# Third recurrence unit in flight, longer stretches between chain looks, norms of the recurrence output on chip: one fp32 four-layer kernel

## The chip, the cores and the metric

One NeuronCore of one Trainium2 chip runs the whole program. The metric is the device time of one execution in microseconds (us); the kernel before was run three times, and its median stands below. TensorE is called PE, VectorE DVE, ScalarE ACT, GpSimd POOL and SyncE (which issues the DMAs) SP, as in the profile.

## The reference, cut to what matters

The input has 512 tokens of width 1024. Two "first" layers are followed by two "second" layers. The change touches the first layers alone, so only these are shown.

```python
for l in range(2):
    h = rmsnorm(x, norm1_g[l])
    p = h @ w_in[l]                       # rw, ret, sg, gate columns
    y_rw  = rwkv7_branch(p_rw, ...)       # recurrence over 512 steps, 8 heads of 64
    y_ret = retention_branch(p_ret, cos, sin)
    y_sg  = sgu_branch(p_sg, ...)
    proj  = einsum('bsgc,gcd->bsgd', stack([y_rw, y_ret, y_sg]), w_branch[l])
    gates = sigmoid(gate_logits)
    x = x + sum(gates * proj, over the branches) @ w_out[l]
    x = x + conv_ffn(rmsnorm(x, norm2_g[l]), ...)

# rwkv7_branch: per step and head
#   S = S diag(w_t) - (S kk_t)(a_t kk_t)^T + v_t k_t^T ;  y_t = S r_t
# and behind it, per head of 64 columns:
y = (y - mean) * rsqrt(var + 64e-5) * lnx_g + lnx_b
y = y + sum(r * k * r_k) * v
y_rw = y * g
# retention_branch ends with, per head of 128 columns:
y = y * rsqrt(mean(y * y) + 1e-6);  y_ret = y * silu(g)
```

## The kernel before

Everything lies features on partitions: a tile is 128 features by 512 tokens. Every projection is a sum over blocks of 128 input features, and every such block is three matmuls (`mm3`, L165 to L170): operands are split into a high and a low part, and high by high, low by high and high by low are summed in PSUM. `weights` (L151 to L161) loads 512 KB of weights (`wraw`, two buffers); ACT makes the high part (`whi`, L159) and DVE the low part (`wlo`, L160). One tile of 1024 input features is 8 blocks, 24 matmuls of 512 columns. Weight tiles that must come out with tokens on partitions go through `tm_group` (L379): four token groups of 256 columns, each needing both halves (chunks) of the weights.

The order of PE's work in the mixing stage of a first layer is written by hand. `Plan` (L68 to L103) keeps threads, Python generators that emit instructions and yield a `Step` with a cost and a wait in a model time. A dense thread (rank 1: input projections, rank 2: retention and gating unit, rank 3: the merge gates) is taken when no chain thread is due; chain threads (rank 0) carry the recurrence and interrupt a dense tile wherever it yields `MORE`. Before, `fm_steps` (L369) yields it after every second block. On the other engines a scheduler orders the work; weight splits and PSUM evacuations have priority, and what stands in `late()` is issued only behind the last evacuation.

The recurrence is done in this way. `rw_pair` (L465) makes the key, decay and rate tiles of one pair of heads; it sums squares (`psk`), sends the sums through DRAM to spread them over the partitions (`sums`, L196: four small matmuls, a copy, a DMA out, two DMAs back), and goes on with `kkr` (L523 or L529) and the products `psA` (L542). `rwkv_inverse` solves small triangular systems on DVE. Then 16 units follow (4 pairs of 4 chunk groups, `rw_unit` L610): transposes `pst`, products `psam`, which DVE masks into `am` (L652, four instructions), `psv`, `psg`, `psh` and `rhs` (L670), `psu`, then `psy` and `psx`. Two `lane` threads (L594) take units from one list, so two units are in flight, each with tiles of its own. Behind the last unit of a pair comes `rw_final` (L706): a scan over six steps (`psz`, L719 and L721), `psY`, then the mean and the reciprocal root of the variance. Both of these go through `sums` and DRAM (`psmean`, `psq`, names `sumd` and `rdw` in the trace), and the result is scaled, shifted, gated (`psgate`, L747) and split into the tiles that the merge reads (`split`, L181 and L182).

Retention (L761) rotates q and k (`ev`, `swp`; `swp` is filled by four DMAs), and per head makes `pssc`, `pret`, `psret`, and a norm `psrn` whose sums go through DRAM too; `ret_end` (L822) multiplies `yret` by the spread result `sqr`.

PSUM has 8 banks: 2 for dense tiles (`pm`), 4 for the recurrence (`pw`), 2 for retention and gating (`pf`). `merge` (L923) runs after the plan: for every block c of 128 output features it multiplies the three branch outputs (n = 0 retention, 1 gating unit, 2 recurrence, by `ORDER1`) with their weights (`pbr`, 12 matmuls a tile), and gates them (L939). The weight stream has the same order (`merge_stream`, L1907).

Of the kernel before, what the change touches and what calls it, by code (L numbers as in the profile page):

```python
# [45 lines left out]
LANES = 2  # L46
# [13 lines left out]
def Dense(cost):  # L60
    return Step(cost)


MORE = Step(1.4, inner=True)
TILE = Dense(1.4)


class Plan:  # L68
# [38 lines left out]
class Kern:  # L107
# [262 lines left out]
    def fm_steps(self, ws):  # L370

        ps = self.PM(name="pm")
        for k in range(KD):
            self.mm3(ps, next(ws), self.h[k], k == 0, k == KD - 1)
            if k % 2 and k < KD - 1:
                yield MORE
        return ps

    def tm_group(self, src, evac):  # L379

        ws = [self.weights(src[i], 1024) for i in range(2)]
        for g in range(4):
            ps = self.PM([128, 512])
            for k in range(KD):
                w = ws[k // 4]
                o = (k % 4) * 256
                hh = (self.h[k][0][:, g * 128:(g + 1) * 128], self.h[k][1][:, g * 128:(g + 1) * 128])
                self.mm3(ps[:, :256], hh, (w[0][:, o:o + 256], w[1][:, o:o + 256]), k == 0, k == KD - 1)
                if k == KD // 2 - 1:
                    yield MORE  # L390
            evac(g, ps[:, :256])
            yield MORE if g < 3 else TILE

# [191 lines left out]
    def rwkv_out(self, l):  # L585
# [4 lines left out]
        self.states, self.left, self.ended = {}, [4] * 4, [False] * 4  # L590
        for i in range(LANES):
            self.plan.add(self.lane(l, i), 0, 2.0 * i)

    def lane(self, l, i):  # L594

        while self.units:
# [7 lines left out]
            yield from self.rw_unit(f, g, self.states[f], i)  # L604
# [4 lines left out]
    def rw_unit(self, f, g, st, lane):  # L609
# [8 lines left out]
        small = lambda shape, name: self.ap.tile(shape, F32, name=name, tag=name, bufs=LANES)  # L618
# [6 lines left out]
        tk = small([128, 2, 128], "tk")  # L625
        nc.vector.tensor_copy(tk, pst[:, 1:3, :])
        vp = self.vp[lane]
        nc.scalar.activation(vp[:, 0:4:3, :], pst[:, 3, :].rearrange("p (e v) -> p e v", e=2), AF.Copy)
        rhs = small([128, 2, 128], "rhs")
        nc.scalar.activation(rhs[:, 0, 64:128], pst[:, 0, 0:64], AF.Copy, scale=-1.0)  # L630
        nc.scalar.activation(rhs[:, 1, 0:64], pst[:, 0, 64:128], AF.Copy, scale=-1.0)
        tt = small([128, 2, 4, 32], "tt")
# [6 lines left out]
        am = self.am[lane]  # L639
# [13 lines left out]
        yield Chain(1.4, 4.0)  # L653
# [10 lines left out]
        gs_ = small([128, 2, 128], "gsb")  # L664
# [6 lines left out]
        yield Chain(0.5, 2.5)  # L671
# [3 lines left out]
        uw = small([128, 2, 128], "uw")  # L675
# [31 lines left out]
    def rw_final(self, l, f, st):  # L707
# [16 lines left out]
        for c in range(1, 8):  # L724
            cs = slice(64 * c, 64 * c + 64)
            for e in range(2):
# [7 lines left out]
        mean = flat(st["cc"])  # L734
# [13 lines left out]
        gt = mean  # L748
# [1326 lines left out]
```

## Time and profile before

| what | us |
|---|---|
| runs, median of 3 (lowest, highest) | 3331.58 (3329.52, 3349.09) |
| the profiled execution, by the same clock | 3336.96 |
| its span in the trace | 3335.3 |
| first merge matmul (`pbr`) of first layer 0, in the trace | 499.34 |
| first merge matmul of first layer 1, in the trace | 1473.06 |

The span is the time between the first and last recorded instruction of the profiled execution. Busy time of an engine counts its instructions alone, not the issue of DMAs. A row of the timeline gives the start, the duration, the engine, the line, the operation with output and input tiles, the shape, a count of like instructions, and in brackets the idle time ahead of it with what ended it. PE's instructions overlap, so the pace is read from the distance of starts, not from durations.

### The profile page before, as it was taken

How to read it: one execution, taken by the hardware profiler on the slowest of the kernel's cores; microseconds unless marked ns; L12 is line 12 of the kernel's file. 1: busy time of each engine (PE TensorE's matmuls, PEld its weight loads, DVE VectorE, ACT ScalarE, POOL GpSimd, SP SyncE). 2: the span in 40 equal slices, each digit the busy share in tenths (PEclk: the TensorE clock that was granted, in tenths of full speed). 3: DMA queues.
4: the chain of work that ended last, by engine and by line, in shares of the span. 5: the costliest groups of instructions: out<-in, count | busy, mean ns of one | idle time of the engine just before them, and what ended most of it. 6: DMA issues, size and time to landing. Idle time of an engine off the chain costs nothing.

```text
span 3335.3 us, 47337 instructions
## 1 busy us (share of the span) xinstructions
PE 3245.5 (97%) x17944; PEld 2596.1 (78%) x17944; DVE 2194.4 (66%) x4062; ACT 1365.3 (41%) x2440; POOL 116.7 (3%) x139
## 2 busy tenths in 40 slices
PE   8999999999999999999999999999999999999998
PEld 6787877888887687878888877876787888777776
DVE  6765656777437755656677456986666669866665
ACT  5433433444335333434444334344334443543343
POOL 0000000000000000000000000010003100100031
PEclk9999999999999999999999999999999999999999
DMA  4433245332433323245333436453455554544464
GB/s 146 124 93 93 79 136 173 124 103 96 136 110 107 120 78 89 83 147 176 101 96 103 146 115 195 141 155 98 120 185 195 171 165 130 156 114 122 150 208 141
DMA packets 200244, 435.41 MB, mean 131 GB/s; under 512 B 29768, under 2 KB 57800, under 8 KB 200016
## 3 DMA queue, kind: packets, MB, share of 16 engines
q1 hardware_dynamic: 200016, 432.38, 41.9%
q8 instruction: 142, 2.33, 0.3%
q14 instruction: 86, 0.70, 0.1%
HBM read 339.57 MB, written 61.49 MB: 120 GB/s over the span
## 4 chain that ended last, share of the span: by engine, by line
PE 85%; DVE 6%; DMA 5%; ACT 2%; issue 1%; SPq 1%; POOL 0%; DVEq 0%; ACTq 0%; POOLq 0%
PE pm L168 22%; PE pm L170 21%; PE pm L169 21%; PE psy L1152 2%; PE pbr L168 2%; PE pbr L169 2%; PE pbr L170 2%; PE pspt L1142 2%; DVE wlo L160 2%; PE psl L1124 1%; DMA rdw<-sumd 1%; PE psl L1125 1%; DMA sqr<-sumd 1%; PE pssc L804 1%; DMA zd<-z 1%
## 5 line engine op out<-in xcount | busy, mean ns | idle before, releaser
L168 PE MATMUL pm<-shi,whi 128*128 128x512 f32 x3072 | 1234.6, 402 | 8.5 <-ACT whi L159 7.4
L170 PE MATMUL pm<-shi,wlo 128*128 128x512 f32 x3072 | 1211.5, 394 | 2.3 <-DVE wlo L160 2.2
L169 PE MATMUL pm<-slo,whi 128*128 128x512 f32 x3072 | 1210.9, 394 | 0.9 <-DVE slo L185 0.9
L159 ACT ACTIVATE whi<-wraw 128x1024 fp32r<-128x1024 f32 x480 | 508.4, 1059 | 887.8 <-PE pm L169 579.0
L160 DVE TENSOR_TENSOR wlo<-wraw,whi 128x1024 fp32r<-128x1024 f32 x480 | 588.7, 1226 | 203.3 <-ACT whi L159 199.4
L168 PEld LDWEIGHTS pm<-shi,whi 128*128 128x128 f32 x3072 | 579.2, 189 | 150.0 <-issue 26.8
L170 PEld LDWEIGHTS pm<-shi,wlo 128*128 128x128 f32 x3072 | 578.9, 188 | 131.1 <-DVE wlo L160 6.8
L169 PEld LDWEIGHTS pm<-slo,whi 128*128 128x128 f32 x3072 | 579.6, 189 | 119.2 <-issue 4.3
L424 DVE TENSOR_TENSOR ev<-pm,rb 128x512 f32<-128x512 f32 x140 | 96.1, 686 | 112.7 <-PE pm L170 112.2
L894 DVE TENSOR_TENSOR gate<-pm,rb 128x512 f32<-128x512 f32 x80 | 55.1, 689 | 121.6 <-PE pm L170 121.3
L168 PE MATMUL pbr<-shi,whi 128*128 128x512 f32 x288 | 116.6, 405 | 12.2 <-ACT shl L181 9.6
L168 PE MATMUL pm<-whi,shi 128*128 128x256 f32 x384 | 115.0, 300 | 10.0 <-ACT whi L159 10.0
L169 PE MATMUL pm<-wlo,shi 128*128 128x256 f32 x384 | 112.0, 292 | 4.8 <-DVE wlo L160 4.8
L170 PE MATMUL pbr<-shi,wlo 128*128 128x512 f32 x288 | 114.3, 397 | 0.0
L169 PE MATMUL pbr<-slo,whi 128*128 128x512 f32 x288 | 114.3, 397 | 0.0
L170 PE MATMUL pm<-whi,slo 128*128 128x256 f32 x384 | 111.6, 291 | 0.0
L939 DVE SCALAR_TENSOR_TENSOR gate<-gate,pbr 128x512 f32<-128x512 f32 x128 | 85.8, 683 | 37.5 <-PE pbr L170 36.3
L943 POOL TENSOR_TENSOR gate<-gate 128x512 f32<-128x512 f32 x48 | 77.4, 1613 | 607.7 <-DVE gate L939 343.8
L936 ACT ACTIVATE gate<-gate 128x512 f32<-128x512 f32 x128 | 75.7, 625 | 42.6 <-DMA gate<-gtd 39.6
L1109 ACT ACTIVATE p<-psl,st 128x256 f32<-128x256 f32 (+3 forms) x128 | 64.9, 511 | 51.6 <-DVE st L1107 44.1
L168 PEld LDWEIGHTS pm<-whi,shi 128*128 128x128 f32 x384 | 76.0, 198 | 12.9 <-ACT whi L159 10.7
L169 PEld LDWEIGHTS pm<-wlo,shi 128*128 128x128 f32 x384 | 76.4, 199 | 6.2 <-DVE wlo L160 5.7
(483 smaller groups left out, 4461.3 us busy)
## 6 DMA issues: line engine op xcount, KB each, us to landing
wraw<-in_w_gt SPq DMA_DIRECT2D x148, 512.0 KB, 3.7
wraw<-in_w_in SPq DMA_DIRECT2D x116, 512.0 KB, 3.6
wraw<-in_f_up SPq DMA_DIRECT2D x88, 512.0 KB, 3.5
gtd<-gate SPq DMA_DIRECT2D x116, 256.0 KB, 2.0
gate<-gtd SPq DMA_DIRECT2D x116, 256.0 KB, 4.0
wraw<-in_w_br SPq DMA_DIRECT2D x44, 512.0 KB, 3.6
wraw<-in_f_dn SPq DMA_DIRECT2D x44, 512.0 KB, 3.5
wraw<-in_w_out SPq DMA_DIRECT2D x32, 512.0 KB, 3.9
```

The costliest lines, as they stand in the source:

```text
L159: nc.scalar.activation(hi[:, :n], raw[:, :n], AF.Copy)
L160: nc.vector.tensor_tensor(lo[:, :n], raw[:, :n], hi[:, :n].bitcast(F32), op=OP.subtract)
L168: nc.tensor.matmul(ps, lhsT=lhs[0], rhs=rhs[0], start=first, stop=False, skip_group_check=skip)
L169: nc.tensor.matmul(ps, lhsT=lhs[0], rhs=rhs[1], start=False, stop=False, skip_group_check=skip)
L170: nc.tensor.matmul(ps, lhsT=lhs[1], rhs=rhs[0], start=False, stop=last, skip_group_check=skip)
L424: self.last = self.nc.vector.tensor_tensor(t, ps, self.rb, op=OP.mult)
L936: nc.scalar.activation(g, g, AF.Tanh, scale=0.5)
L939: nc.vector.scalar_tensor_tensor(g, g, 1.0, pb, op0=OP.add, op1=OP.mult)
L943: (nc.gpsimd if self.pre and n in self.cfg.get("pa", (1, 2, 3)) else nc.vector).tensor_tensor(g, g, acc, op=OP.add)
L1109: nc.scalar.activation(p[:, :w], l, AF.Exp, bias=st[:, 0:1], accum_out=st[:, 1:2])
L1142: nc.tensor.transpose(pt_[:, b * 128:(b + 1) * 128], ps[e][:, b * 128:(b + 1) * 128], self.ident)
L1152: nc.tensor.matmul(psy[64 * e:64 * e + 64, :], lhsT=vs[e][b], rhs=pts[e][:, b * 128:(b + 1) * 128], start=first and b == 0, stop=last and ...
```

## The change

It does nine things, all in the first layers.

1. `LANES` is 3. The third lane's tiles come from tiles that are free by then (tags C4 and R); POOL zeroes two of them. Lanes start 0, 10 and 20 us apart in the plan's model time, not 0 and 2.
2. `fm_steps` yields `MORE` once, after four blocks, and `MORE` and `TILE` count 2.75, not 1.4.
3. A chain thread is taken up to 0.8 us (`NEAR`) before it is due.
4. Some of a unit's waits in the plan are shorter (4.0 to 3.2, 2.5 to 2.0, 2.5 to 2.2).
5. Two pairs of ACT copies into `rhs` become one copy each.
6. `tm_group` works chunk by chunk: all four groups with the first half of the weights, then all with the second. Two groups share a PSUM bank, and both `pm` banks are held all along.
7. `rw_final` norms on the chip: two matmuls with 64 equal weight columns put the sums on all partitions at once (`psm`, 512 columns each), four small ones make the sums of squares (`psq`, 2 columns), ACT and DVE make the reciprocal root of 8 columns (`hcol`), and eight matmuls spread it (`rows`, 64 by 128). Two round trips through DRAM are gone, and three DVE instructions behind the root become two.
8. The wait behind `psm` is 3.0 where the two waits behind the trips were 10.0 and 11.0.
9. The merge takes branch 2 of block c behind branches 0 and 1 of block c+1, and the weight stream follows.

```diff
-LANES = 2
+LANES = 3
-MORE = Step(1.4, inner=True)
-TILE = Dense(1.4)
+MORE = Step(2.75, inner=True)
+TILE = Dense(2.75)
+NEAR = 0.8
...
-            due = sorted((th for th in self.threads if th["chain"] and th["due"] <= self.t), key=lambda th: th["due"])
+            due = sorted((th for th in self.threads if th["chain"] and th["due"] <= self.t + NEAR), key=lambda th: th["due"])
...
-            if k % 2 and k < KD - 1:
+            if k == KD // 2 - 1:
                 yield MORE
...
     def tm_group(self, src, evac):
-        ws = [self.weights(src[i], 1024) for i in range(2)]
-        for g in range(4):
-            ps = self.PM([128, 512])
-            for k in range(KD):
...
+        ps = [self.PM([128, 2, 256]) for _ in range(2)]
+        for i in range(2):
+            w = self.weights(src[i], 1024)
+            for g in range(4):
+                for k in range(4):
...
+                    self.mm3(ps[g // 2][:, g % 2], hh, ww, i == 0 and k == 0 and g % 2 == 0, i == 1 and k == 3, skip=True)
+                if i:
+                    evac(g, ps[g // 2][:, g % 2])
+                if g % 2 and (i, g) != (1, 3):
                     yield MORE
...
-            self.plan.add(self.lane(l, i), 0, 2.0 * i)
+            self.plan.add(self.lane(l, (self.lanes + [third])[i]), 0, 10.0 * i)
...
-        nc.scalar.activation(rhs[:, 0, 0:64], psv[:, 0, :], AF.Copy, scale=-1.0)
-        nc.scalar.activation(rhs[:, 1, 64:128], psv[:, 1, :], AF.Copy, scale=-1.0)
-        yield Chain(0.4, 2.5)
+        nc.scalar.activation(seats["rhs"].rearrange("p (a t) -> p a t", a=4)[:, 0:4:3, :], psv, AF.Copy, scale=-1.0)
+        yield Chain(0.4, 2.0)
...
-        self.sums(y0, self.sel[:, 0], 2, self.P([128, 128], "psmean"), mean,
-                  lambda t, ps: nc.scalar.activation(t, ps, AF.Copy, scale=-1.0 / 64))
-        yield Chain(0.4, 10.0)
-        with self.late():
-            nc.vector.tensor_tensor(y0, y0, mean, op=OP.add)
+        psm = self.P(name="psmean")
+        for e in range(2):
+            nc.tensor.matmul(psm[64 * e:64 * e + 64, :], lhsT=self.sel[:, 0, e:e + 1].to_broadcast([128, 64]), rhs=y0,
+                             start=True, stop=True, skip_group_check=True)
+        nc.vector.scalar_tensor_tensor(y0, psm, -1.0 / 64, y0, op0=OP.mult, op1=OP.add)
         sq = rdw
         nc.scalar.activation(sq, y0, AF.Square)
-        yield Chain(0.0, 3.0)
-        self.norms(sq, self.sel[:, 0], 2, self.P([128, 128], "psq"), bias=self.eps[:, 1:2], scale=1.0 / 64)
...
-        yield Chain(1.6, 11.0)
-        with self.late():
-            nc.vector.tensor_tensor(y0, y0, sq, op=OP.mult)
-        nc.vector.tensor_scalar(y0, y0, v(V_LG + f), v(V_LB + f), op0=OP.mult, op1=OP.add)
-        nc.vector.tensor_tensor(y0, y0, bv, op=OP.add)
+        yield Chain(2.0, 3.0)
+        psq = self.P([128, 8], "psq")
+        for g in range(4):
+            nc.tensor.matmul(psq[:, 2 * g:2 * g + 2], lhsT=sq[:, g * 128:(g + 1) * 128], rhs=self.sel[:, 0, 0:2],
+                             start=True, stop=True)
+        col = self.ap.tile([128, 16], F32, name="hcol", tag="hcol", bufs=1)
+        nc.scalar.activation(col[:, 8:16], psq, AF.Sqrt, bias=self.eps[:, 1:2], scale=1.0 / 64)
+        nc.vector.reciprocal(col[:, 0:8], col[:, 8:16])
+        yield Chain(0.5, 2.0)
+        psr = self.P(name="psr")
+        self.rows(psr, col, 2, 64)
+        nc.vector.scalar_tensor_tensor(y0, y0, v(V_LG + f), psr, op0=OP.mult, op1=OP.mult)
+        nc.vector.scalar_tensor_tensor(y0, y0, v(V_LB + f), bv, op0=OP.add, op1=OP.add)
         nc.vector.tensor_tensor(y0, gt, y0, op=OP.mult)
...
+def merge_order(nb):
+
+    if nb != 3:
+        return [(c, n) for c in range(8) for n in range(nb)]
+    o = []
+    for c in range(9):
+        o += [(c, 0), (c, 1)] * (c < 8) + [(c - 1, 2)] * (c > 0)
+    return o
```

The instructions of DVE around the first 256-column group of layer 0 (retention's values), in the kernel before; `ev` from `pm` is the evacuation of the rotated key's tile, `swp` its half-swapped copy that comes by DMA, `wlo` a weight split.

```order
147 L518 SCALAR_TENSOR_TENSOR mix<-mix,vec_219,e_1070 128x512
148 L489 RECIPROCAL sums<-sums 128x128
149 L424 TENSOR_TENSOR ev<-pm,rb 128x512
150 L780 TENSOR_TENSOR swp<-swp,sin 128x512
151 L781 TENSOR_TENSOR ev<-ev,cos 128x512
152 L160 TENSOR_TENSOR wlo<-wraw,whi 128x1024
153 L782 TENSOR_TENSOR ev<-ev,swp 128x512
```

The same place in the changed kernel.

```order
147 L523 SCALAR_TENSOR_TENSOR mix<-mix,vec_229,e_1061 128x512
148 L790 TENSOR_TENSOR swp<-swp,sin 128x512
149 L791 TENSOR_TENSOR ev<-ev,cos 128x512
150 L429 TENSOR_TENSOR ev<-pm,rb 128x512
151 L164 TENSOR_TENSOR wlo<-wraw,whi 128x1024
152 L792 TENSOR_TENSOR ev<-ev,swp 128x512
153 L557 TENSOR_TENSOR sqk<-sqk,mix 128x512
```

The evacuation from `pm` stands behind the two rotation instructions on `swp` now, and before it stood ahead of them.

DVE at the end of retention's fourth head in layer 0, before; `yret<-yret,sqr` is that head's last multiplication, `cc` the scan of a pair, `rhs` the second step of a unit.

```order
384 L721 SCALAR_TENSOR_TENSOR cc<-psz,ds,cc 128x64
385 L424 TENSOR_TENSOR gate<-pm,rb 128x512
386 L160 TENSOR_TENSOR wlo<-wraw,whi 128x1024
387 L721 SCALAR_TENSOR_TENSOR cc<-psz,ds,cc 128x64
388 L822 TENSOR_TENSOR yret<-yret,sqr 128x512
389 L670 TENSOR_TENSOR rhs<-psh,rhs 128x256
390 L721 SCALAR_TENSOR_TENSOR cc<-psz,ds,cc 128x64
391 L670 TENSOR_TENSOR rhs<-psh,rhs 128x256
```

The same place in the changed kernel, where `tk` and `am` of three units stand side by side.

```order
385 L639 COPY tk_215<-pst 128x256
386 L639 COPY tk_224<-pst 128x256
387 L186 TENSOR_TENSOR shl<-y_1661,shl 128x512
388 L639 COPY sm<-pst 128x256
389 L726 SCALAR_TENSOR_TENSOR cc<-psz,ds,cc 128x64
390 L832 TENSOR_TENSOR yret<-yret,sqr 128x512
391 L660 TENSOR_TENSOR am_211<-psam,c_rwmask 64x4x64 x2
392 L164 TENSOR_TENSOR wlo<-wraw,whi 128x1024
393 L660 TENSOR_TENSOR am_211<-psam,c_rwmask 64x4x64 x2
394 L660 TENSOR_TENSOR am_220<-psam,c_rwmask 64x4x64 x4
395 L660 TENSOR_TENSOR am<-psam,c_rwmask 64x4x64 x4
```

Behind the multiplication by `sqr` now stand the twelve masks of three units and a weight split; before, two `rhs` steps and a scan step stood there.

DVE from the last pair's output to the merge of layer 0, before; `y` is the pair, `gate<-gate,pbr` the merge.

```order
529 L214 RECIPROCAL sums<-sums 128x128
530 L939 SCALAR_TENSOR_TENSOR gate<-gate,pbr 128x512 x2
531 L943 TENSOR_TENSOR gate<-gate 128x512
532 L160 TENSOR_TENSOR wlo<-wraw,whi 128x1024
533 L752 TENSOR_TENSOR y_3681<-y_3681,rdw 128x512
534 L753 TENSOR_SCALAR y_3681<-y_3681,vec_219 128x512
535 L754 TENSOR_TENSOR y_3681<-y_3681,xt 128x512
536 L755 TENSOR_TENSOR y_3681<-cc,y_3681 128x512
537 L939 SCALAR_TENSOR_TENSOR gate<-gate,pbr 128x512
538 L182 TENSOR_TENSOR shl<-y_3681,shl 128x512
```

And in the changed kernel.

```order
533 L759 RECIPROCAL hcol<-hcol 128x8
534 L763 SCALAR_TENSOR_TENSOR y_3483<-y_3483,vec_229,psr 128x512
535 L764 SCALAR_TENSOR_TENSOR y_3483<-y_3483,vec_229,xt 128x512
536 L765 TENSOR_TENSOR y_3483<-cc,y_3483 128x512
537 L429 TENSOR_TENSOR gate<-pm,rb 128x512
538 L186 TENSOR_TENSOR shl<-y_3483,shl 128x512
539 L164 TENSOR_TENSOR wlo<-wraw,whi 128x1024
540 L429 TENSOR_TENSOR gate<-pm,rb 128x512
541 L164 TENSOR_TENSOR wlo<-wraw,whi 128x1024
542 L947 SCALAR_TENSOR_TENSOR gate<-gate,pbr 128x512 x2
```

The pair's output is split before the first `pbr` is gated, with gate tiles (`gate<-pm`) still to come, and before it came after three of them.

Counted in the written order of PE in layer 0 up to the first `pbr`, the dense matmuls are as many as before (1584), the chain matmuls 917 (893 before), and the places where PE leaves the dense work for a chain 84 (115 before). The last pair's `psr` has 36 dense matmuls behind it ahead of the first `pbr`.

## Rows read from the trace of the kernel before

**Rows 1.** The page: busy time, share of the span and instructions of each engine.
```profile
PE 3245.5 (97%) x17944; PEld 2596.1 (78%) x17944; DVE 2194.4 (66%) x4062; ACT 1365.3 (41%) x2440; POOL 116.7 (3%) x139
```

**Rows 2.** Waits of PE, 20 to 1600 us: us in total, times, longest.
```profile
PE pbr L168 <- ACT shl L181: 9.6, 2, 5.0
PE pm L168 <- ACT whi L159: 8.6, 2, 5.1
PE pm L169 <- DVE wlo L160: 4.1, 2, 2.3
PE psu L674 <- DVE rhs L670: 3.9, 2, 3.3
PE psA L542 <- DVE kkr L529: 3.5, 4, 1.5
```

**Rows 3.** Timeline of PE: two chain visits amid dense work.
```profile
193.51 0.55 PE L656 MATMUL psv<-vp,am 128*128 128x64 f32 x4
193.88 0.48 PE L168 MATMUL pm<-shi,whi 128*128 128x512 f32 x1
194.19 0.39 PE L169 MATMUL pm<-slo,whi 128*128 128x512 f32 x1
194.42 0.39 PE L170 MATMUL pm<-shi,wlo 128*128 128x512 f32 x1
...
197.78 0.55 PE L656 MATMUL psv<-vp,am 128*128 128x64 f32 x4
...
198.59 0.48 PE L168 MATMUL pm<-shi,whi 128*128 128x512 f32 x1
```

**Rows 4.** Windows: first 256-column group; both merge starts; behind a wait.
```profile
core 0: us, PE busy (x) PEld busy (x) DVE busy (x) ACT busy (x) POOL busy (x), PEclk, DMA share, GB/s
115.93:136.66 20.73, 14.86 (x105) 14.13 (x104) 13.62 (x24) 10.62 (x19) 0.00 (x0) 0.84 0.39 112
499.34:530.00 30.66, 26.02 (x106) 20.54 (x105) 18.72 (x26) 12.55 (x17) 0.00 (x0) 0.94 0.45 140
1473.10:1504.00 30.90, 25.91 (x101) 20.40 (x100) 17.71 (x24) 12.28 (x17) 0.00 (x0) 0.89 0.43 133
1316.90:1320.30 3.40, 3.40 (x19) 3.06 (x18) 0.79 (x2) 0.38 (x1) 0.00 (x0) 0.50 0.00 0
```

**Rows 5.** Timeline of PE: a sums visit.
```profile
482.88 0.42 PE L200 MATMUL psmean<-y,sel 128*32 128x128 f32 x8
483.23 0.50 PE L168 MATMUL pm<-shi,whi 128*128 128x512 f32 x1
```

**Rows 6.** Timeline of PE: four column sums of one column.
```profile
18.61 0.95 PE L310 MATMUL psn<-ones,sq 128*128 128x1 f32 x8
19.42 0.49 PE L169 MATMUL pm<-slo,whi 128*128 128x512 f32 x1
```

**Rows 7.** Timeline of PE in a second layer: products of 64 output rows.
```profile
2200.45 1.15 PE L1152 MATMUL psy<-pt,vf 128*64 128x128 f32 x16
2201.53 0.33 PE L1124 MATMUL psl<-hi 128*128 128x128 f32 x1
```

**Rows 8.** Timelines of PE and DVE: fourth head's norm, layers 0 and 1.
```profile
330.33 0.43 PE L200 MATMUL psrn<-sqr,sel 128*32 128x128 f32 x8
...
342.96 0.69 DVE L822 TENSOR_TENSOR yret<-yret,sqr 128x512 f32<-128x512 f32 x1 [5.41 <-DMA sqr<-sumd]
...
1299.84 0.42 PE L200 MATMUL psrn<-sqr,sel 128*32 128x128 f32 x8
...
1315.26 0.69 DVE L822 TENSOR_TENSOR yret<-yret,sqr 128x512 f32<-128x512 f32 x1 [8.20 <-DMA sqr<-sumd]
```

**Rows 9.** Lines by form, 20 to 535 us: the masks of a unit.
```profile
L652 DVE TENSOR_TENSOR am<-psam,c_rwmask 64x256 f32<-64x256 f32 x64 | 26.9, 420 | 1.7 <-PE psam L647 0.6
```

**Rows 10.** Timeline of DVE at the first 256-column group of layer 0.
```profile
119.45 0.63 DVE L424 TENSOR_TENSOR ev<-pm,rb 128x512 f32<-128x512 f32 x1
...
121.29 0.69 DVE L780 TENSOR_TENSOR swp<-swp,sin 128x512 f32<-128x512 f32 x1 [1.21 <-DMA swp<-ev]
```

More of the change, by code (lines that the diff above doesn't have):

```diff
@@ L45 @@
 HALF = object()
-LANES = 2
+SMALL = ("tk", "rhs", "tt", "gsb")
+LANES = 3
 class Step:
@@ L590, in rwkv_out, with lane @@
         self.states, self.left, self.ended = {}, [4] * 4, [False] * 4
+        am, sm, uv = self.tile("C4", (128, 2, 4, 128), name="am"), self.tile("C4", (128, 4, 256), name="sm"), self.tile("R", name="uv")
+        vp = uv[:, 0:256].rearrange("p (a v) -> p a v", a=4)
+        nc = self.nc
+        nc.gpsimd.memset(am.rearrange("p e m t -> p (e m t)"), 0.0)
+        nc.gpsimd.memset(uv[:, 0:256], 0.0)
+        third = dict(am=am, vp=vp, uw=uv[:, 256:512], **dict((n, sm[:, i, :]) for i, n in enumerate(SMALL)))
         for i in range(LANES):
-            self.plan.add(self.lane(l, i), 0, 2.0 * i)
-    def lane(self, l, i):
+            self.plan.add(self.lane(l, (self.lanes + [third])[i]), 0, 10.0 * i)
+    def lane(self, l, seats):
         while self.units:
@@ L607, in lane, with rw_unit @@
                 self.plan.add(self.rw_final(l, f, self.states[f]), 0, 2.0)
-    def rw_unit(self, f, g, st, lane):
+    def rw_unit(self, f, g, st, seats):
         nc = self.nc
@@ L617, in rw_unit @@
         u0 = f * 8 + g
-        small = lambda shape, name: self.ap.tile(shape, F32, name=name, tag=name, bufs=LANES)
+        tk, rhs, gs_, uw = [seats[n].rearrange("p (a t) -> p a t", a=2) for n in ("tk", "rhs", "gsb", "uw")]
+        tt = seats["tt"].rearrange("p (u b t) -> p u b t", u=2, b=4)
+        am, vp = seats["am"], seats["vp"]
         pst = self.P([128, 4, 128], "pst")
@@ L925, in merge @@
         nb = len(ys)
[L926 removed]
+        s, late, acc = [], [], {}
         ws = self.stream(wbr[l])
[L928 to L947 removed]
+        for c, n in merge_order(nb):
+            if (c, n) in self.gd:
+                g = self.F(name="gate")
+                nc.sync.dma_start(g, self.gd[c, n])
+            else:
+                g = self.gate(self.gs, "F")
+            nc.scalar.activation(g, g, AF.Tanh, scale=0.5)
+            pb = self.fm_tile(ws, ys[n], name="pbr")
+            with self.tc.high_priority(offset=self.cfg.get("hp", self.AHEAD)):
+                nc.vector.scalar_tensor_tensor(g, g, 1.0, pb, op0=OP.add, op1=OP.mult)
+            if late and n == self.cfg.get("ln", 1):
+                s.append(self.split(late.pop(), *stag(len(s)), scale=0.5))
+            if c in acc:
+                (nc.gpsimd if self.pre and n in self.cfg.get("pa", (1, 2, 3)) else nc.vector).tensor_tensor(
+                    g, g, acc[c], op=OP.add)
+            acc[c] = g
+            if n == nb - 1:
+                self.dump("%ss%d_%d" % (self.pre, l, c), g)
+                late.append(acc.pop(c))
+        for t in late:
+            s.append(self.split(t, *stag(len(s)), scale=0.5))
         self.begin_norm()
@@ L1904, with merge_stream @@
 ORDER1 = [1, 2, 0]
-def merge_stream(w):
+def merge_order(nb):
[5 more added lines that the diff above has]
+    return o
+def merge_stream(w, order=None):
     t = []
-    for c in range(8):
-        for n in range(w.shape[0]):
-            t += list(w[n][:, c * 128:(c + 1) * 128].reshape(-1, 128, 128))
+    for c, n in order or [(c, n) for c in range(8) for n in range(w.shape[0])]:
+        t += list(w[n][:, c * 128:(c + 1) * 128].reshape(-1, 128, 128))
     return np.stack(t).reshape(-1, 8, 128, 128).transpose(0, 2, 1, 3).reshape(-1, 128, 1024)
@@ L2022, in layout @@
                            for l in range(L)])
-    o["w_br1"] = np.stack([merge_stream(I["w_branch"][l][ORDER1]) for l in range(L)])
+    o["w_br1"] = np.stack([merge_stream(I["w_branch"][l][ORDER1], merge_order(3)) for l in range(L)])
     o["w_out1"] = np.stack([np.stack(_fm(I["w_out"][l], range(0, 1024, 128))) for l in range(L)])
```

66 lines of the change are left out of this document (17 added, 49 removed).

## The prediction

> **What bounds the kernel now.** I read the busy times first: PE works 97% of the span, DVE 66%, ACT 41% [rows 1]. PE sets the end, and it has little idle time to give back, so an edit is worth what it takes from PE's waits, adds to PE's work, or costs at a lowered clock. Second I read PE's waits over both mixing stages [rows 2]: five rows hold 29.7 us. 9.6 us of it is the start of the merge, where the recurrence's last tile is late; 12.7 us (8.6 + 4.1) is the first 256-column group, which needs two fresh weight tiles at once; the rest is 3.9 us on `rhs` and 3.5 us on `kkr`. Third I read the granted clock in windows around these waits: it falls to 0.84 on the mean around the first 256-column group, 0.94 and 0.89 around the merge starts, and is 0.50 (the 1.2 GHz level) for 3.4 us right behind the `psu` wait of layer 1 [rows 4]. The longest waits of the table, 3.3 to 5.1 us, are where the clock falls in these windows, so I price such a wait at itself plus half of the half-speed stretch behind it. The windows give up 20.73 x 0.16 = 3.3 us, 30.66 x 0.06 = 1.8 us and 30.90 x 0.11 = 3.4 us of full-speed time. Part of it lies in the waits themselves; outside them I take 2.6 us for each first group and 4.1 us for both merge starts. So the starts of the merge lose 9.6 + 4.1 = 13.7 us and the first groups 12.7 + 5.2 = 17.9 us, over both layers.
>
> A visit to a chain amid dense work is the other thing that the change cuts. Dense matmuls start 0.23 us apart (194.19 to 194.42). `psv` alone takes 0.37 us (193.51 to 193.88), `psv` with `psg` 0.81 us (197.78 to 198.59) [rows 3]: two steps in one visit cost twice one step, so the row shows no price of the visit itself beside its steps.
>
> **The sum.** I go by the profiled execution, 3336.96 us, which is 5.4 us above the median of the runs, 3331.58; one per cent is 33 us, and that is about what a measurement of this kernel can tell from no change.
>
> *Start of the merge, -13.7.* In the new order the last `psr` has 36 dense matmuls behind it and then four `pbr` tiles of 12 matmuls that need no recurrence output (branches 0 and 1 of two blocks): 84 x 0.23 = 19 us. Needed in that time are two fused DVE instructions, the gating, and the split, about five 0.7 us instructions of the length of those in [rows 8, 10], some 4 us. The wait goes, and nothing else is late there in the order. If the cover were gone the 13.7 us would come back.
>
> *Norms of the recurrence on chip, +18.2.* Eight finals, four in each layer. Each loses two sums visits of 0.35 us (482.88 to 483.23 [rows 5]). It gains `psm`, two products of 64 output rows by 512 columns; `psr`, eight of 64 rows by 128 columns; and `psq`, four of 2 columns. The trace has no `psm`, but the nearest row streams the same 1024 columns in eight products of 64 rows: 1.08 us (2200.45 to 2201.53 [rows 7]). I take 1.08 for `psr` (the same shape) and 1.08 for `psm`. `psq` is like the four column sums of the first norm, 0.81 us (18.61 to 19.42 [rows 6]). So 1.08 + 1.08 + 0.81 - 0.70 = 2.27 us a final, 18.2 us for eight. All of it is on PE, which has no slack. Below: if `psq` takes half of its row and `psm` and `psr` 0.9 each, 2.21 - 0.70 a final, 12 us; above: if the two halves of `psm` do not run beside each other, 2.16, and each visit adds a little, 25 us. The waits of the finals on DMAs go, but these were covered by other threads except at the merge start, which is counted.
>
> *`sqr` with three lanes behind it, +11.* In both kernels DVE runs in order, and the multiplication of the fourth head waits for a DMA that lands 12.6 us after `psrn` in layer 0 (330.33 to 342.96) and 15.4 us in layer 1 (1299.84 to 1315.26); DVE is idle 5.4 and 8.2 us in front of it [rows 8]. Before, PE lost the `psu` wait of 3.9 us [rows 2] and the half clock behind it in layer 1, 1.7 us [rows 4], with about 0.5 us more, 6 us in all. In the new order that multiplication stands ahead of the masks of three units, written side by side. PE reaches the fifth `psam` bank some 8 us after `psrn` (48 matmuls of 256 columns at half of 0.23 us, 5.5, then transposes, a scan step and four `psam`), has only four banks, and gets the next after the landing, the multiplication (0.69) and two masks of 0.42 [rows 9]: 12.6 + 1.5 - 8 = 6 us. Then it runs into the last masks once more, 1 us, and pays half clock for 3.4 us, 1.7 us. So 8.5 us a layer, 17 for both, against 6: +11. Below: -6, if the landing is early enough that nothing waits (the two trips through DRAM that are gone make the queues emptier). Above: +25, if layer 1 keeps 15.4 us and the clock stays low longer.
>
> *First 256-column group and `psA`, 0.* Chunk by chunk, the group needs only the first weight tile at its start, so the 17.9 us could go. But DVE's order now puts the evacuation that frees the second `pm` bank behind the two instructions on `swp`. Before, it ran at 119.45, while the `swp` instruction started at 121.29 after waiting for its DMA [rows 10]; the group needs that bank 24 such matmuls, 2.8 us, after its start. Since DVE there waits for a landing that comes some 5 us after the group starts (115.93 is where I put its start, 121.29 the landing), PE waits for about 3 to 5 us and pays half clock behind it; and two chunks of weights still have to be split by ACT and DVE in a stretch where DVE is busy 13.62 of 20.73 us [rows 4]. I leave the loss where it was: 0, between -18 (all of it goes) and +8 (a wait at every one of two banks).
>
> *Smaller edits.* A third of the `kkr` and `psret` waits may go with other distances in the plan: -1.5. One ACT copy instead of two, twice a unit, is off PE's path: ACT is 41% busy [rows 1]. Its table loads for the root in each final and the third lane's start: +1. The later looks (after four blocks instead of two) delay each chain step by up to 2.7 us; the third lane and the 0.8 us of grace are what covers that. Without them a pair would end later, by 6 steps of a scan and 8 of a unit, and the merge's 19 us of cover would take up to 15 us of it. I cost it at 0.
>
> Sum: -13.7 + 18.2 + 11 + 0 - 1.5 + 1 = +15, so 3336.96 + 15 = 3352 in an execution like the profiled one, and 3331.58 + 15 = 3346 as the median.
>
> **Rivals.** *The stalls go (15%).* The `swp` DMA lands before its instruction is reached and the `sqr` result too, since the finals no longer use SP's queue. Then the first group gives -18 and the multiplication gives -5 instead of +11, the sum is -13.7 + 18.2 - 18 - 5 - 0.5 = -19, and the time 3312. For it speaks that two trips of three DMAs each vanish from the queue with every final; against it that the landing before took 15.4 us in layer 1 with the same transfers around it.
>
> *Fewer visits pay (13%).* There are 31 fewer visits a layer, 62 in all. If each saved 0.2 us, as much as half of the 0.37 us of one `psv` visit, that is -12.4 us and the time is 3334. Against it stand the two visits of [rows 3], where one with two steps cost 0.81 and one with one 0.37. The Trainium skill, in "TensorEngine Tiling (Array Packing)", section Key Properties, says "Mode switching requires drain: Changing tiling mode (not just tile) drains the TensorE". By that rule a visit with smaller tiles costs something beyond its steps, the change would save it 62 times, and `psm` and `psr` would pay it eight times each; the visits of [rows 3] have full-array tiles and cannot show it.
>
> *Slower by over 1% (14%).* One mechanism: a DVE instruction that waits for a DMA stands ahead of what PE needs, with three units behind it and four banks. If the landing stays over 13 us behind `psrn` in both layers (15.4 was seen), PE waits 15.4 + 1.5 - 8 = 9 us and more with half clock for two stretches, 3.4 us, that is 5 more a layer than in my sum, +10; and if the same happens at the two `pm` banks of the first group, a wait of 4 us and its half clock, +8. The sum is then 15 + 10 + 8 = +33, the time 3365. It decides from a landing of 13 us on.
>
> *The change doesn't act (8%).* The third lane may never run beside the others, since DVE serves one unit's masks after another; then only the norms and the merge order are left, +18.2 - 13.7 = +4.5, and the time is 3336.
>
> **How the numbers follow.** My forecast has 50%: 3346, with 3334 to 3358 as its own range from the norms' bounds (-6 to +7) and half of those of `sqr`. The range reaches to the rivals on both sides, from 3308 (stalls gone, a little more) to 3372 (the slow case with 7 us of norm cost on top), and leaves out about 15%. Faster by over 1% needs 3298 and is out of reach of every case but the first with fewer visits on top: 3%. Slower by over 1% is the third rival, 14%. Within 1%: 83%.
>
> **What would show it.** Right: no wait of PE on `shl` at the merge; visits of `psm`, `psq`, `psr` of 1.1, 0.8 and 1.1 us; a wait of PE on `am` behind `yret<-yret,sqr` of over 4 us with a stretch at 0.50; a wait of `pm` on an `ev` at the first 256-column group. Wrong: a DVE that never idles at `sqr`; no half-speed stretch in the mixing stages; dense tiles that start closer together than before. The forecast fails if the two stretches where I expect waits have none, or if `psm` or `psr` take over 2 us.

## The result, and the profile after

The changed kernel took 3380.13 us (median of 4, 3378.18 to 3382.36) beside 3333.64 us for the kernel before on the same chips: a ratio of 1.013, 95% interval 1.0109 to 1.015. It is slower by 1.3%, 46 us where 15 were forecast, and lies above the forecast's upper end of 3372. The profiled execution has a span of 3379.7 us.

The page's first part and PE's waits, 20 to 1650 us, of the changed kernel (us in total, times, longest):

```profile
PE 3271.3 (97%) x18040; PEld 2615.1 (77%) x18040; DVE 2188.3 (65%) x4054; ACT 1354.9 (40%) x2364; POOL 118.8 (4%) x143
...
PE psam L655 <- DVE am L660: 14.1, 4, 6.5
PE psA L547 <- DVE kkr L534: 9.4, 4, 3.1
PE pm L172 <- DVE ev L429: 5.8, 2, 3.0
PE psv L664 <- DVE rdw L693: 5.5, 2, 3.2
PE pm L172 <- ACT vret L798: 4.5, 8, 0.6
PE pm L172 <- ACT vsg L849: 4.5, 8, 0.6
```

The row of `shl` at the merge and the rows of `whi` and `wlo` [rows 2] are gone. In their place PE waits in the middle of the recurrence, on masks, on `kkr`, on `rdw`, and on the copies that empty the shared banks of a 256-column group. The shares of busy time [rows 1] hardly show it.

The same windows as [rows 4] at the two merge starts, then both mixing stages whole, then the stretch of the fourth head's norm in layer 0 (a window's row gives its length, then each engine's busy time with its instructions, the granted clock of PE, and the DMAs' share and rate):

```profile
core 0: us, PE busy (x) PEld busy (x) DVE busy (x) ACT busy (x) POOL busy (x), PEclk, DMA share, GB/s
530.09:560.75 30.66, 30.66 (x133) 24.82 (x132) 19.91 (x25) 13.01 (x16) 0.00 (x0) 1.00 0.55 157
1522.29:1553.20 30.91, 30.91 (x135) 25.01 (x134) 19.96 (x26) 13.01 (x16) 0.00 (x0) 1.00 0.52 157
...
20.00:530.09 510.09, 484.49 (x3320) 383.12 (x3319) 307.48 (x580) 194.70 (x370) 2.95 (x5) 0.97 0.30 94
1022.00:1522.29 500.29, 474.38 (x3280) 374.62 (x3280) 301.94 (x565) 189.74 (x364) 2.94 (x5) 0.98 0.31 94
...
342.00:358.00 16.00, 7.89 (x71) 6.75 (x71) 7.18 (x15) 2.81 (x3) 0.00 (x0) 0.66 0.19 47
```

Both mixing stages of the kernel before:

```profile
20.00:499.34 479.34, 468.73 (x3272) 371.10 (x3271) 307.03 (x579) 198.23 (x405) 0.84 (x1) 0.99 0.34 104
1000.00:1473.06 473.06, 459.41 (x3225) 363.35 (x3223) 300.35 (x562) 192.56 (x398) 0.63 (x1) 0.99 0.34 104
```

PE is busy all through the merge starts at full clock, and from the first to the last `pbr` a merge takes 66.7 us, twice, where it took 73.4 and 74.7: that part came as forecast, with 14.7 us gained. The loss lies in the mixing stages, which are 31 and 27 us longer. Over both, PE idles 27 us more and is busy 31 us more; 17 us of the latter are the work of the norms (below), and the rest stands beside a lower clock, 0.97 and 0.98 for 0.99.

Around the fourth head PE does 7.9 us of work in 16 us, at 0.66 of full clock on the mean. The rows behind it, from the timelines of PE and DVE:

```profile
333.80 0.43 PE L204 MATMUL psrn<-sqr,sel 128*32 128x128 f32 x8
...
347.94 0.69 DVE L832 TENSOR_TENSOR yret<-yret,sqr 128x512 f32<-128x512 f32 x1 [8.18 <-DMA sqr<-sumd]
348.55 0.85 DVE L660 TENSOR_TENSOR am<-psam,c_rwmask 64x256 f32<-64x256 f32 x2
...
349.55 0.69 PE L655 MATMUL psam<-kr,kkr 64*64 64x128 f32 x4 [6.52 <-DVE am L660]
...
1329.09 0.42 PE L204 MATMUL psrn<-sqr,sel 128*32 128x128 f32 x8
...
1342.27 0.69 DVE L832 TENSOR_TENSOR yret<-yret,sqr 128x512 f32<-128x512 f32 x1 [7.22 <-DMA sqr<-sumd]
...
1343.88 0.69 PE L655 MATMUL psam<-kr,kkr 64*64 64x128 f32 x4 [5.57 <-DVE am L660]
```

In layer 0 DVE idles 8.18 us for the landing, which comes 14.1 us behind `psrn`; the masks stand behind it, and PE's fifth `psam` waits 6.52 us for a bank. In layer 1 the landing comes 13.2 us behind `psrn`, and PE waits 5.57 us. These rows answer to [rows 8].

The norms of a final, from PE's timeline in three places of layer 0:

```profile
332.78 1.09 PE L196 MATMUL psr<-c_ident,hcol 128*64 128x128 f32 x16
333.80 0.43 PE L204 MATMUL psrn<-sqr,sel 128*32 128x128 f32 x8
...
512.28 1.08 PE L741 MATMUL psmean<-y,sel 128*64 128x512 f32 x4
513.29 1.12 PE L749 MATMUL psgate<-mix,gup 128*128 128x512 f32 x2
...
517.03 0.95 PE L755 MATMUL psq<-sel,rdw 128*128 128x2 f32 x8
517.84 0.47 PE L172 MATMUL pm<-shi,whi 128*128 128x512 f32 x1
```

From start to next start `psr` takes 1.02 us, `psmean` (the `psm` of the forecast) 1.01 and `psq` 0.81, 2.84 in all. Without the two sums visits, 0.70, that is 2.14 us a final, 17 us for eight.

### The profile page after: what moved, and what is told of

It is laid out like the page before. It is cut to its first block, busy times and chain, and to the rows that moved or that the text cites. A ratio compares the mean times of both kernels' runs of the same rounds, so it can differ in the third digit from the quotient of the medians.

```text
span 3379.7 us, 47346 instructions
## 1 busy us (share of the span) xinstructions
PE 3271.3 (97%) x18040; PEld 2615.1 (77%) x18040; DVE 2188.3 (65%) x4054; ACT 1354.9 (40%) x2364; POOL 118.8 (4%) x143
## 4 chain that ended last, share of the span: by engine, by line
PE 84%; DVE 6%; DMA 5%; ACT 2%; issue 2%; SPq 1%; POOL 0%; DVEq 0%; ACTq 0%; POOLq 0%
PE pm L172 21%; PE pm L174 21%; PE pm L173 21%; PE pbr L172 2%; PE pbr L174 2%; PE pbr L173 2%; PE psy L1163 2%; PE pspt L1153 2%; DVE wlo L164 1%; DMA sqk<-sumd 1%; PE psl L1135 1%; PE psl L1136 1%; DMA sumd<-sums 1%; ACT whi L163 1%; PE pssc L814 1%
## 5 line engine op out<-in xcount | busy, mean ns | idle before, releaser
L904 DVE TENSOR_TENSOR gate<-pm,rb 128x512 f32<-128x512 f32 x80 | 55.1, 689 | 125.6 <-PE pm L174 125.3
L429 DVE TENSOR_TENSOR gate<-pm,rb 128x512 f32<-128x512 f32 x48 | 33.1, 691 | 70.9 <-PE pm L174 70.7
```

The source lines that it names most:

```text
L429: self.last = self.nc.vector.tensor_tensor(t, ps, self.rb, op=OP.mult)
```

## The experiments

Every run stands beside the kernel before on the same chip; a ratio is the run's time over that of the kernel before, with its 95% interval. Medians of the kernel before lay between 3334.7 and 3338.2 us. Theory 1: DVE instructions that wait for a DMA stand ahead of what PE needs. Theory 2: the third lane crowds. Theories 3 and 4: the looks cost by bunching chain steps, or the visits themselves cost.

**Undoing one part of the changed kernel.** First DVE's order alone.

```diff
-        nc.vector.tensor_tensor(rhs, psh, rhs, op=OP.add)
+        self.last = nc.vector.tensor_tensor(rhs, psh, rhs, op=OP.add)
...
-                self.plan.add(self.ret_end(l, h, y, sq), 0, 12.0)
+                self.plan.add(self.ret_end(l, h, y, sq), 0, 24.0)
```

The results of `am` and `xt` are marked in the same way, so that `late()` puts the multiplication behind them.

> The changed kernel, with the multiplication by sqr issued on DVE behind the second step (rhs) of the units that stood behind it; the order of PE is the same, row for row. Theory 1 (a DVE instruction that waits for a DMA holds up what PE needs, and the half clock behind it makes it dearer): the waits of PE on am and on rdw go, about 19.9 us on am with their half-clock tails and 8.6 us on rdw with theirs, so 3380 falls to 3350, 3345 to 3358. Theory 2 (three units side by side crowd PSUM and DVE, whatever waits for a DMA): the waits stay or move, 3375 to 3380.

3373.63 us, 1.011 (1.0086 to 1.0134). The wait on `am` fell from 14.1 to 4.1 us, but `rdw` rose to 7.5 us, because another instruction with the same fault came to the head of DVE's queue (timelines of DVE and PE in this run; the `rdw` instructions stand behind `swp`):

```profile
213.90 0.69 DVE L790 TENSOR_TENSOR swp<-swp,sin 128x512 f32<-128x512 f32 x1 [3.07 <-DMA swp<-ev]
...
216.70 0.91 PE L664 MATMUL psv<-uv,am 128*128 128x64 f32 x4 [3.14 <-DVE rdw L693]
```

The intervals of this run and of the changed kernel overlap: the mechanism is seen in the rows, and its 17 us were not won back.

Then `rw_final` as before (a diff is not shown; it is that of the change, turned round).

> The changed kernel with the old rw_final: mean and root through DRAM again. Theory 1: PE has 18.4 us less to do in the eight finals and the merge's new order still covers the last pair in part, so 3362 (3358 to 3370). Theory 2 (the norms on chip are worth their PE time because the trips hold the lanes up): the trips come back as waits of PE at the merge or of lanes, and the time stays at 3375 to 3390.

3370.34 us, 1.0101 (1.0077 to 1.0125): about 10 us less than the changed kernel, with intervals that overlap, though PE has 17 us less to do. The merges take 22 us more: 78.9 and 76.8 us from first to last `pbr` where the changed kernel has 66.7 twice.

The lanes:

```diff
-        for i in range(LANES):
-            self.plan.add(self.lane(l, (self.lanes + [third])[i]), 0, 10.0 * i)
+        for i in range(2):
+            self.plan.add(self.lane(l, (self.lanes + [third])[i]), 0, 2.0 * i)
```

> The changed kernel with two lanes, 2 us apart as before. Theory 1: the DMA wait of DVE stays, but with eight masks instead of twelve behind it and PE having other work; the wait on am shrinks by a third, 3370 to 3378. Theory 2 (crowding by the third lane): all waits on am, rdw and psh go, 3350 or below. A third reading: two lanes end later and the merge waits again, over 3385.

3363.68 us, 1.008 (1.0055 to 1.0105), between the two theories. The wait of `psam` on `am` is gone, and one of 9.8 us at `psx`, behind ACT's `cc`, came. With the looks as they are in the change, the third lane and its start so cost some 17 us. Next the looks, whole and by halves.

```diff
-MORE = Step(2.75, inner=True)
-TILE = Dense(2.75)
-NEAR = 0.8
+MORE = Step(1.4, inner=True)
+TILE = Dense(1.4)
+NEAR = 0.0
...
-            if k == KD // 2 - 1:
+            if k % 2 and k < KD - 1:
```

> The changed kernel with looks every two blocks, costs of 1.4 and no early taking of chains, as before. Theory 1: the looks are not what costs; waits move, 3370 to 3385. Theory 3 (chains looked at too late make the units late): most of the added waits go, 3345 to 3360. Theory 4 (each visit costs PE something of its own): the visits come back, and the time rises to 3390 or more.

3348.72 us, 1.0036 (1.0025 to 1.0047): 31 us of the 46 go with the looks alone undone. Theory 4 falls: the visits came back, and the time fell. Both mixing stages of this run:

```profile
20.00:515.50 495.50, 478.10 (x3321) 378.49 (x3320) 307.55 (x580) 196.28 (x373) 3.57 (x5) 0.99 0.32 96
1009.30:1492.80 483.50, 468.26 (x3272) 370.45 (x3271) 301.26 (x563) 190.44 (x365) 2.96 (x5) 0.99 0.31 97
```

The merges stay at 66.7 us. Beside the kernel before, PE is busy 18 us more, about the work of the norms, and idles 8 us more. Beside the changed kernel it idles 19 us less and is busy 12.5 us less, and the wait of `psam` on `am` is 0.9 us where it was 14.1.

Only `NEAR = 0.0`:

> The changed kernel without the early taking of chains (NEAR 0), looks still after four blocks. If taking a step early is what makes PE wait: 3348 to 3360. If the distance between the looks is: 3372 to 3390, or more.

3361.8 us, 1.0075 (1.006 to 1.009). Only the looks every two blocks at 1.4, `NEAR` kept:

> The changed kernel with looks every two blocks at a cost of 1.4, chains still taken 0.8 us early. If the distance between the looks is what costs: 3343 to 3355, as the run with both undone. If the early taking is: 3370 to 3385.

3402.52 us, 1.0202 (1.0183 to 1.0221), slower than the changed kernel. The two halves don't add: by the ratios, -31 us with both undone, -18 with the one, +24 with the other.

A second difference is mixed into some of these runs. `MORE` and `TILE` also count the looks inside `tm_group`. Before, `tm_group` looks after 12 matmuls of 256 columns, and changed it looks after 24, which the prediction reads as 2.8 us; so 1.4 fits the one and 2.75 the other. Where the changed `tm_group` runs with 1.4 (the looks undone, the looks every two blocks, and the runs with the chunks below), the model time of the plan runs at half of PE's time in the groups, and chain steps are written late. Where the old one runs with 2.75 (the two runs below with one look a tile), it runs twice as fast, and they are written early. The runs that change `NEAR` alone are free of this.

**One part on the kernel before.** The three looks edits together:

> The kernel before with the looks alone: one look a tile, after four blocks, the model cost of a look 2.75, chains taken up to 0.8 us early. Theory 3 (the later looks bunch chain steps, so that DVE and ACT get them all at once and PE waits): slower without any of the other edits, 3350 to 3365. Theory 3b (they cost only with three lanes or with the norms on chip beside them): 3330 to 3342.

3363.97 us, 1.0083 (1.0068 to 1.0098): they need no third lane to cost 28 us, the miscount in the groups included. The wait on `shl` at the merge is 2.0 us, less than before (9.6). The early taking alone:

```diff
-            due = sorted((th for th in self.threads if th["chain"] and th["due"] <= self.t), key=lambda th: th["due"])
+            due = sorted((th for th in self.threads if th["chain"] and th["due"] <= self.t + 0.8), key=lambda th: th["due"])
```

> The kernel before with one edit: chains taken up to 0.8 us early, looks every two blocks at 1.4 as before. If a step written early makes PE stand at it, whatever the lanes: slower, 3350 to 3390, with waits of PE at psA on kkr and at steps of the units. If it costs only with the other edits: 3331 to 3342.

3368.14 us, 1.0093 (1.0078 to 1.0108). PE's waits in this run:

```profile
PE psA L542 <- DVE kkr L529: 17.1, 6, 4.1
PE psv L656 <- DVE am L652: 8.5, 6, 3.5
PE psret L809 <- DVE pret L807: 8.0, 4, 4.0
```

PE stands at steps whose inputs are not there: `kkr` 17.1 us where [rows 2] has 3.5. One look after four blocks alone, chains when due:

> The kernel before with one look a tile, after four blocks, at a cost of 2.75, and chains taken only when due. If the early taking is the whole cost: 3331 to 3342. If the distance of the looks costs by itself: 3345 to 3362.

3380.11 us, 1.0132 (1.0117 to 1.0148), as much as the whole change, from other places. Two rows of PE's waits:

```profile
PE pbr L168 <- ACT shl L181: 12.0, 2, 6.1
PE psq L200 <- ACT rdw L741: 10.4, 2, 5.7
```

The last pair is later for the merge: 12.0 us on `shl`, 9.6 before, and the merges take 79.1 and 79.9 us from first to last `pbr`, 11 us more than before. The greater part of the loss lies ahead of them, in the mixing stages; both waits of `psq` stand inside the gating unit's 256-column groups, where the plan's time is wrong in this run. So it does not show what the distance of the looks costs by itself.

Chains later instead of earlier (`th["due"] + 0.8 <= self.t`, and a plan without dense work steps on to that time):

> The kernel before with chains taken 0.8 us after they are due at the earliest (the early taking with its sign turned). If the written order's slack is what PE pays for when it is missing, and there is still some missing before: the small waits of chains (kkr, rhs, am, about 8 us) go, 3325 to 3335. If the kernel before has slack enough: no change, 3333 to 3342; if units get late and the merge waits longer: over 3345.

3356.31 us, 1.0062 (1.0047 to 1.0077). The waits in the recurrence shrank (the rows of `kkr` at `psA` and of `rhs` at `psu` are gone), and the merges took more than that back (89.8 and 88.4 us from first to last `pbr`):

```profile
PE pbr L168 <- ACT shl L181: 22.3, 2, 11.2
```

So the wait in the plan is a trade: early, PE stands at a step; late, the last pair holds up the merge.

**The merge and the groups.** The new merge order on the kernel before (the diff's last part):

> The kernel before with the merge's new order alone: branch 2 of a block one block later, and the weight stream with it. By the sum the two waits of 9.6 us and the half clock behind them go: 3335 falls by 13.7 to 3322 (3319 to 3326). Rival (the wait only moves to the second block's gating, or the gate transfers are late in the new order): 3331 to 3338.

3328.06 us, 0.9979 (0.9969 to 0.9989): faster by 7 us. A wait of 5.5 us at `pbr` stays, on DVE's gating. In DVE's order that gating stands behind the last pair's product with its norm, which still comes through DRAM (DVE's timeline of this run):

```profile
511.40 0.69 DVE L752 TENSOR_TENSOR y<-y,rdw 128x512 f32<-128x512 f32 x1 [4.27 <-DMA rdw<-sumd]
512.01 0.68 DVE L937 SCALAR_TENSOR_TENSOR gate<-gate,pbr 128x512 f32<-128x512 f32 x1
```

Then `tm_group` chunk by chunk on top of it:

> The kernel before with the merge's new order and tm_group chunk by chunk. Beside the merge order alone (-8): if the first group's wait for two weight tiles goes and nothing comes in its place, -17.9 more, 3310; by the forecast's zero, 3328; if the shared banks wait for copies of ACT and evacuations of DVE at every group, 3335 to 3345.

3352.72 us, 1.0053 (1.0035 to 1.0071): the chunks cost 25 us, with their looks counted at half of their time. The wait of 8.3 us for `whi` went, and these rows came (PE's waits, then the timelines of DVE, ACT and PE at one of them):

```profile
PE psy L682 <- ACT cc L705: 6.5, 2, 4.1
PE psx L698 <- ACT cc L705: 5.6, 2, 2.9
PE pm L168 <- DVE ev L425: 4.6, 2, 2.8
...
PE pm L168 <- ACT vret L789: 4.5, 8, 0.6
PE pm L168 <- ACT vsg L840: 4.5, 8, 0.6
...
215.18 0.69 DVE L823 TENSOR_TENSOR yret<-yret,sqr 128x512 f32<-128x512 f32 x1 [4.64 <-DMA sqr<-sumd]
...
216.72 0.27 ACT L688 ACTIVATE y<-psy 64x128 f32<-64x128 f32 x1 [5.30 <-DVE rdw L689]
...
217.30 0.47 PE L698 MATMUL psx<-tk,uw 64*64 64x64 f32 x2 [2.71 <-ACT cc L705]
```

A chain of three queues in order: DVE at the head waits 4.64 us for `sqr`, `rdw` stands behind it; ACT's copies wait 5.30 us for `rdw`; PE waits 2.71 us for the bank that ACT's `cc` empties. PE's row names ACT, and the cause is a DMA.

**Between the two kernels.** The changed kernel with the looks and `rw_final` as before leaves the third lane (with its shorter waits and single copies), the chunks and the merge order:

> The changed kernel with the looks, their cost and the taking of chains as before, and rw_final through DRAM as before: what is left is the third lane, the chunks of tm_group and the merge order. Beside the 3349 of the run with the looks undone it shows the price of the norms: by their PE time -18.4, and a part of the merge's wait back, +5, so 3335 (3328 to 3342). If the norms are hidden or pay in another place: 3345 to 3355.

3355.03 us, 1.0056 (1.0039 to 1.0073), the same as the merge order and the chunks without a third lane (1.0053). So with the looks of before the third lane costs and gives nothing that can be told. Beside the run with only the looks undone (1.0036) PE does 17 us less here for the norms, and the time is no shorter: it is 7 us longer, which is about what the two intervals leave open.

**Looking for a better kernel.** The merge order with the norms on chip for the last pair alone (`if f == 3:` around the new code):

> The kernel before with the merge's new order and the norms on chip for the last pair alone (the other three through DRAM). The last pair is early enough then that the merge's wait goes whole (-13.7 against the -8 of the order alone), for two finals of 2.3 us: 3336 - 13.7 + 4.6 = 3327 (3322 to 3332). Rival: the last pair waits elsewhere, as with the order alone or worse, 3330 to 3336.

3333.35 us, 0.9983 (0.9973 to 0.9992). The merges fell to 66.7 and 67.2 us, and a wait of 4.6 us at a `psq` came in layer 1. The time cannot be told from that of the order alone: the first `pbr` of layer 0 starts at 502.9 us, with the order alone at 498.4. The same finals with the third lane, the chunks, the looks of before and `sqr` late:

> The changed kernel with the looks as before, norms on chip for the last pair alone, and the multiplication by sqr behind the rhs and xt of the units. By the sum against the run with the looks undone: six finals fewer, -13.8, and the waits on ACT at the second 256-column group that stood behind sqr, -9.9 with their half clock -6: 3320 to 3330. If the third lane costs by itself: 3335 to 3350.

3354.38 us, 1.0052 (1.0037 to 1.0067), no better than with all norms through DRAM (1.0056). Late chains with the merge order:

> The merge's new order with chains 0.8 us late. If both add: 3318 to 3328. If late chains bring the merge's wait back: 3330 to 3340.

3344.13 us, 1.0031 (1.0021 to 1.0042): the merges still wait. With the last pair's norms on chip as well:

> The kernel before with the merge's new order, chains 0.8 us late, and the norms on chip for the last pair alone. If slack in the written order is what PE pays for, and the last pair's lateness was the only price of late chains: the mixing stages keep 936 us or so (two finals of 2.3 us included), the merges fall to 134 to 140 us, and the time is 3336 - 14 - 12 = 3310 (3302 to 3318). If the merges still wait: 3320 to 3340.

3333.24 us, 0.9992 (0.9983 to 1.0001): no difference. The first to last `pbr` took 75.6 us in both layers, for the last pair's scan now lies inside the merge. And the multiplications by `sqr` on POOL (`nc.gpsimd` for `nc.vector` in `ret_end`), with the merge order:

> The merge's new order alone, and the eight multiplications of yret by sqr on POOL, which is idle there; PE's order is the same, row for row, as in the run with the merge order alone (3328 beside 3336 for the kernel before). If a DVE that waits for a DMA is what holds PE up there: the waits on rhs and on am (2.4 and 1.0 us) and the half clock behind them go, 3322 to 3327. If DVE's wait is covered in that order: 3326 to 3331. If POOL's slower product is late for the splits that the merge reads: over 3331.

3332.01 us, 0.9992 (0.9983 to 1.0001): nothing beyond the merge order. PE's wait of 2.4 us on `rhs` is gone, and it was worth too little to tell. No run is measurably faster than the merge order alone, which is 0.2% faster than the kernel before.

## Why the prediction was wrong

The steps of one path from the kernel before to the changed one, each the difference of two ratios above (times 3335 us; each ratio is uncertain by some 3 to 7 us, and on another path the shares differ, as the halves of the looks show; the miscount in the groups comes in with the chunks and goes with the looks):

| step | forecast | measured |
|---|---|---|
| merge order | -13.7 | -7 |
| `tm_group` by chunks | 0 | +25 |
| third lane, shorter waits, single copies | +11, -1.5, +1 | +1 |
| norms on chip | +18.2 | -7 |
| looks after four blocks, up to 0.8 us early | 0 | +31 |
| sum | +15 | +43 |

**The start of the merge** was right for the whole change: the merges gained 14.7 us. The order alone gives half, for the gating waits behind the last pair's trip through DRAM. That the order and the norms of the last pair together bring the merges to 66.7 and 67.2 us is shown; that the program gains more by both than by the order alone is not.

**The norms** were right as PE work (2.14 us a final measured, 2.27 forecast). As a price they are not settled: with the trips through DRAM back, PE's 17 us did not come off the time beside the run with the looks undone (-7 in the table, which the noise can make), and about 10 us of them did beside the whole change, with overlapping intervals. "All of it is on PE, which has no slack" overlooked how much of the merge's gain hangs on the norms: 22 us of longer merges came with the trips in the second case.

**`sqr` with three lanes** was right in mechanism and wait: landings 14.1 and 13.2 us behind `psrn` (12.6 and 15.4 were used), waits of 6.5 and 5.6 us (6 was worked out), half clock behind them. Its size in time is not settled: moved away, it uncovered the wait on `swp`; with two lanes it is gone, and some 17 us with it, beside other changes of the order. With the looks of before it is 0.9 us, and the third lane costs nothing that can be told. So this term hung on the looks, which the prediction had at 0.

**The first group** came half as written. The wait for `whi` and `wlo` went and the wait for `ev` came (5.8 us in two, 3 to 5 us each were forecast). The zero failed through what lies outside the group: 9.0 us of PE at the groups' shared banks, 0.6 us sixteen times, and the shift of later chain steps, which in the run with the chunks put the `sqr` wait of DVE in front of a unit's copies. The bound of +8 was worked out from the group alone; the 25 us measured hold the miscount of the looks too, so the chunks' own price stays open.

**The step that failed most** is "The later looks ... delay each chain step ... I cost it at 0", with the third lane and the 0.8 us of grace as cover. The cover held where it was meant to: with the grace the wait on `shl` is 2.0 us on the kernel before (12.0 without it), and in the changed kernel it is gone. What was put at nothing is the price of the cover. Steps taken 0.8 us early stand in front of inputs that are not there (17.1 us on `kkr`): that costs 31 us alone on the kernel before, and taking the grace out of the changed kernel gives 18 us back. (With one look a tile on the kernel before it pays: 28 us are lost with it, 44 without.) The looks as a whole cost 31 us in the changed kernel, by the run with them undone: 19 us of waits and 12.5 us of busy time at a lower clock, and the wait behind `sqr` comes with them.

**The sum without the looks** came near, and in part by luck: with them undone the kernel is 12 us slower than the one before, where 15 were forecast. The merges (-14.7) and the norms' work (+18) stand there as forecast; in place of the 11 us for `sqr` stand 8 us of other idle time, with 13.0 us of waits for the gating unit's shared banks.

**The rivals.** The slow rival named the mechanism, DVE at a DMA with PE behind it, and put 3365 on it. Its condition came (landings over 13 us in both layers), its wait of 9 us did not (6.5 and 5.6). The changed kernel is 15 us beyond, with waits on `kkr` (9.4 us) and `rdw` (5.5 us) and at the shared banks, which it did not count. The stalls did not go, as the first rival had it, and the change acted, against the last: three units stand side by side at the fourth head. "Fewer visits pay" is not borne out: one look a tile on the kernel before cuts the visits of layer 0 by 21 in the written order and is 45 us slower. The run says nothing on what a switch costs by itself, so what the Trainium skill states in "TensorEngine Tiling (Array Packing)", Key Properties, that a change of the tiling mode drains the engine, stays unweighed here.

What stays open: the price of the looks' distance by itself and that of the chunks, for no run has either with the looks in the groups counted right and all else as before; and how the 31 us divide between the single waits and the half clock behind each.

## What to carry to other kernels

Where the order of one engine is written out with a model of time, a change to that model moves every step behind it, and its cost is not the sum of what the edits do at their own places: ask which in-order queues (here DVE at a landing, ACT behind DVE) will now stand between a step and its input. Steps written 0.8 us earlier cost 31 us and steps written 0.8 us later 21, so such an edit is run alone before it is combined; of the edits run alone here, one was worth keeping. When a part of such a change is undone, look at what else the same constant counts: here it counted the looks of two kinds of work, and the parts could not be priced cleanly. And a stage's end is worth looking at with everything that makes its last input late: the order of the merge took half of the merge's loss away, and the order with the norms of the last pair all of it, though the stage ahead then took longer.

## What the runs showed of the hardware

Half-speed stretches come with the waits: the mean granted clock of the mixing stage of layer 0 is 0.97 over 510 us in the changed kernel and 0.99 over 479 us before. By these rounded figures that is some 10 us more of full-speed time given up, where PE's idle time grew by 15 us. The fourth head's stretch alone gives up 16 x 0.34 = 5.4 us, a part of it in the wait itself. A product of 128 by 512 took 0.69 us on DVE and 1.28 us on POOL (in the run with the multiplications by `sqr` there). Four column sums of 2 columns took PE 0.81 us, as long as those of 1 column [rows 6], and two products of 64 rows by 512 columns 1.01 us, as long as eight of 64 by 128 (1.02).
